# A hybrid decoder trunk on one core: 14 of 16 differential heads' weights transposed by DVE and by way of DRAM

## The chip, the cores and the metric

The kernel runs on one core of a Trainium2 chip. The metric is the device time of one launch in microseconds (us), the median of several runs. Five engines work side by side, each through its own queue in order: PE (TensorE, matmuls; its weight loads are shown as PEld), ACT (ScalarE), DVE (VectorE), POOL (GpSimd) and SP (SyncE). In this kernel SP issues the loads of the weights, and POOL issues most other transfers after the start.

## The reference

The trunk has two layers over 512 tokens of width 2048. In each, one projection of the normed input feeds two groups of eight heads. Group B is a latent attention (MLA). Group A, which the change touches, is a differential attention: each head has two softmax maps over the same values, and their difference weighs the values.

```python
s = jnp.einsum('bqhmd,bkhmd->bmhqk', qb, k).astype(jnp.float32) * scale
...
s = jnp.where((dist >= 0)[None, None, None], s + bias[None, None], NEG_INF)
p = jax.nn.softmax(s, axis=-1)
w = p[:, 0] - lam * p[:, 1]
return jnp.einsum('bhqk,bkhd->bqhd', w.astype(v.dtype), v)
```

The head's output is normed (RMS), scaled, multiplied by a gate, and goes with the other heads' outputs into the output projection. The causal mask means that a block of 128 queries needs only the keys up to its own end.

## The kernel before, in words

**Precision.** Every float32 operand of a matmul is split into a high and a low part of type fp32r: the high one is a cast on ACT, the low one the difference on DVE. A product is three matmuls (`mm3`, L348): high by high, high by low, low by high.

**Weights.** They come in blocks of 128 x 1024 (512 KB) through `WStream` (L62). SP loads `raw` (two buffers), ACT casts `whi` (L104), DVE subtracts to `wlo` (L105), two buffers each. A block is split one block ahead, so the cast waits until PE has left the block before. A block is 24 matmuls of 512 columns.

**Order.** `run_jobs` (L146) walks through a list of jobs, all on PE: projections of 8 steps (`job_proj`, L353), the values' job of 32 steps (`job_v`, L448), parts of the output projection. A step is six matmuls. Attention work is attached to step numbers: `DIFF_AT` (L35) says for a differential head at which steps of its stretch the scores (S), the transposes (T), the products with the values (A) and the norm (F) are issued, for four query blocks (S, T) or key blocks (A). PE, SP and POOL keep this order as written; on ACT and DVE a scheduler may set the order at build time. Each engine then runs its own queue strictly in order, so POOL and SP are not tied to PE's steps: they run ahead until something makes them wait.

**A differential head** h has the jobs z(h) (the gate), q and k of head h+1, and at heads 0 and 4 the values' job for the next four heads, which before the change comes right after z(h). `after` (L57) adds the length of the head's jobs to A and F, so these fall into z(h+1). The steps (L779 to L831):

- `s_step` issues four matmuls into two PSUM banks (tag `s`, two buffers), two softmaxes (`softmax`, L695: DVE L699, ACT L701, DVE L702), scales one map on ACT (L797) and adds the other on DVE (L799). The sum stands in `s1` (tag `sb`, two buffers); `s0` has tag `sa`, two buffers, so the third query block needs the first one's buffers back.
- `t_step` calls `transpose_w` (L705): up to four PE transposes of 128 x 128 into PSUM (L708), ten in a head, then the high part on ACT (L714) and the low part on DVE (L715), into `pth` and `ptl`, one buffer each, which hold the transposed weights of all query blocks.
- `av_step` (L717) issues twelve matmuls in four groups, all of which read `pth` or `ptl`, and at the end prepares the sum of squares (`ones_sum`, tag `kr`, two buffers).
- `fin` is the norm: two matmuls (L342, L343), `rsqrt_of`, two products on DVE (L825, L826), a split.

The last head of each layer has its own steps, `LAST_AT`, since the output projection follows. POOL loads a head's bias at step 0 of the head before it (`load_bias`, L877).

Of the kernel before, what the change touches and what calls it, by code (L numbers as in the profile page):

```python
# [15 lines left out]
P = 128  # L16
T = 512
# [14 lines left out]

MLA_AT = {"S": (2.5, 3.5, 4.5, 7), "T": (5, 7, 9.5, 11), "A": (0.5, 1, 1.5, 5)}
FIRST_AT = {"S": (2.5, 3.5, 8.5, 8), "T": (4.5, 7, 10.5, 11), "A": (0.5, 0.5, 1.5, 5)}
DIFF_AT = {"S": (3, 4, 6, 10), "T": (8.5, 9, 13, 17), "A": (0.5, 1, 2, 2), "F": 5}  # L35
LAST_AT = {"S": (2, 4, 6, 10), "T": (7, 9, 13.5, 17), "A": (18.5, 19, 19.5, 20), "F": 23}


# [124 lines left out]
def trunk(ctx, tc, blocks, xf, gains, diff_lambda, rel_bias_table, onehot, tables, wb, outf):  # L163
# [553 lines left out]
    def av(h, kb):  # L717
# [7 lines left out]
        nc.tensor.matmul(o, vh, h["pl"][:, r], start=False, stop=False)  # L725
        nc.tensor.matmul(o, vl, h["ph"][:, r], start=False, stop=kb == 3)  # L726

    def new_pt(h):
        h["ph"] = t_([P, PTW], F32R, "pth", 1)
        h["pl"] = t_([P, PTW], F32R, "ptl", 1)  # L730
# [46 lines left out]
        return schedule(at, s_step, t_step, av_step)  # L777

    def diff_steps(l, hd, done, at):  # L779
        h = {"e": hd % 4}  # L780

        def s_step(qb):
            def f():
                if qb == 0:
                    h.update(q=st["q"], k=st["k"], b=st["bias"][hd])
                n = (qb + 1) * P
                c = slice(qb * P, (qb + 1) * P)
                p0, p1 = p_("s", 2), p_("s", 2)
                q, (k, kx) = h["q"], h["k"]
                nc.tensor.matmul(p0[:, :n], q[:, 0, c], k[:, 0, :n], start=True, stop=False)  # L790
                nc.tensor.matmul(p1[:, :n], q[:, 1, c], k[:, 1, :n], start=True, stop=False)
                nc.tensor.matmul(p0[:, :n], q[:, 0, c], kx[:, 0, :n], start=False, stop=True)
                nc.tensor.matmul(p1[:, :n], q[:, 1, c], kx[:, 1, :n], start=False, stop=True)
                bias = h["b"][:, 384 - qb * P:]
                s0, m0 = softmax(p0, n, bias, 0.125, "sa")
                s1, m1 = softmax(p1, n, bias, 0.125, "sb")
                nc.scalar.activation(out=s0[:, :n], in_=s0[:, :n], func=AF.Copy, scale=m0[:, 1:2])  # L797
                nc.vector.tensor_tensor(out=m1[:, 1:2], in0=m1[:, 1:2], in1=nlam[:, l:l + 1], op=ALU.mult)
                nc.vector.scalar_tensor_tensor(out=s1[:, :n], in0=s1[:, :n], scalar=m1[:, 1:2], in1=s0[:, :n], op0=ALU.mult, op1=ALU.add)  # L799
                h[qb] = s1  # L800
            return f

        def t_step(qb):
            def f():
                if qb == 0:
                    new_pt(h)
                transpose_w(h, qb, h.pop(qb))
            return f

        def av_step(kb):  # L810
# [17 lines left out]
            split2(m, r)  # L828
            done(m)

        return schedule(at, s_step, t_step, av_step) + [(at["F"], fin)]  # L831


    nlam = sb.tile([P, 120], F32, name="nlam")
# [80 lines left out]
    for l in range(DEPTH):  # L915
# [36 lines left out]
        def v_diff(q, wi=wi):  # L952
            return job_v([b_kouter(wi, C_V + q * T, j) for j in range(8)], lambda kc: (xh[kc], xl[kc]), True)
# [60 lines left out]
        for h in range(NH):  # L1014
            bias = [(0, lambda h=h: [load_bias(i) for i in ((0, 1) if h == 0 else (h + 1,)) if i < NH])]
            jobs = [z_job(C_Z + h * P)]
            if h < NH - 1:
                jobs += ([v_diff(h // 4)] if h % 4 == 0 else []) + d_jobs(h + 1)
                add(jobs, bias, diff_steps(l, h, keep(h), after(DIFF_AT, sum(n for n, _ in jobs))))
            else:  # L1020
                jobs += [job_out_half(l, 0, accs, mslot), job_out_half(l, 1, accs, mslot), job_out_half(l, 2, accs, mslot), job_out_first(l, accs, mslot, last_evac if last else out_evac, spare(0))]
                add(jobs, [(0, load_res(0)), (0, load_res(1)), (22, load_res(2)), (24, load_res(3))] + [(MIX_AT + MIX_ST * i, split_mix(i)) for i in range(8)],
                    diff_steps(l, h, keep(h), LAST_AT))
# [111 lines left out]
```

## Time and profile before

| what | value |
|---|---|
| median of 3 runs | 1797.67 us (1795.96 to 1799.13) |
| the profiled execution's own time | 1796.06 us |
| its span | 1794.3 us |
| PE busy | 1777.7 us, 99% |
| DVE, ACT, POOL busy | 1021.7, 878.4, 41.6 us |
| mean load on the DMA | 101 GB/s |

The profile shows one execution, and its span is 1.76 us shorter than that execution's own time. "Busy" adds up the durations that the profile gives. PE's matmuls are pipelined and overlap: the timeline shows one of 512 columns starting every 0.23 us with a duration of 0.39 us. What an instruction costs PE is therefore read from the starts of its neighbours, not from its duration.

### The profile page before, as it was taken

The page shows a single profiled execution, that of the slowest core. Times are in us where ns is not written, and L with a number is a line of the kernel's source. Part 1 is how long each engine was busy: PE and PEld are TensorE (multiplying, and loading weights), DVE is VectorE, ACT ScalarE, POOL GpSimd, SP SyncE. Part 2 cuts the span into 40 slices and gives each one's busy share as a digit, 9 for nine tenths or more (in the row PEclk, how much of TensorE's full clock was granted, in tenths as well). Part 3 has the DMA queues.
Part 4 walks back from the last instruction along what each step waited for, and adds up shares of the span by engine and source line. Part 5 has one row for each costly group of instructions (what it writes and reads, how often), then busy time and mean ns, then how long its engine had stood idle before and what let it go on. Part 6 is the DMA issues. An engine that isn't in the chain of part 4 may idle for free.

```text
span 1794.3 us, 21822 instructions
## 1 busy us (share of the span) xinstructions
PE 1777.7 (99%) x8341; PEld 1483.6 (83%) x8341; DVE 1021.7 (57%) x1905; ACT 878.4 (49%) x1548; POOL 41.6 (2%) x82
## 2 busy tenths in 40 slices
PE   9999999999999999999999999999999999999997
PEld 7888888888888888888888888888888888888886
DVE  6666646546766477534535655655367745774334
ACT  6455646535555367423434655554256635663331
POOL 0000000000000000001100000000000000000000
PEclk9999999999999999999999999999999999999999
DMA  6342222232322322444432222222332232223343
GB/s 220 99 148 77 65 77 85 85 100 88 91 89 89 103 78 87 129 141 141 141 112 94 82 71 77 79 86 89 99 92 91 77 100 83 90 93 118 118 124 128
DMA packets 55540, 181.13 MB, mean 101 GB/s; under 512 B 6563, under 2 KB 10915, under 8 KB 55436
## 3 DMA queue, kind: packets, MB, share of 16 engines
q1 hardware_dynamic: 48972, 159.10, 28.3%
q0 software_dynamic: 6032, 20.21, 3.8%
q8 instruction: 66, 1.08, 0.3%
q10 hardware_dynamic: 432, 0.43, 0.1%
q14 instruction: 38, 0.31, 0.1%
HBM read 171.30 MB, written 11.03 MB: 102 GB/s over the span
## 4 chain that ended last, share of the span: by engine, by line
PE 97%; DVE 1%; ACT 1%; DMA 0%; issue 0%; SPq 0%; DVEq 0%
PE pacc L349 24%; PE pacc L351 24%; PE pacc L350 24%; PE pacc L464 3%; PE pacc L466 3%; PE pacc L465 3%; PE ptp L708 2%; PE po L725 1%; PE po L726 1%; PE po L724 1%; PE po L464 1%; PE po L466 1%; PE po L465 1%; PE ps L351 1%; PE ps L350 1%; PE ps L349 1%
## 5 line engine op out<-in xcount | busy, mean ns | idle before, releaser
L104 ACT CAST whi<-raw 128x1024 fp32r<-128x1024 f32 (+1 forms) x283 | 292.7, 1035 | 591.5 <-PE pacc L350 412.2
L349 PE MATMUL pacc<-x,whi 128*128 128x512 f32 x1471 | 581.8, 395 | 0.0
L351 PE MATMUL pacc<-x,wlo 128*128 128x512 f32 x1471 | 572.2, 389 | 0.0
L350 PE MATMUL pacc<-x,whi 128*128 128x512 f32 x1471 | 571.8, 389 | 0.0
L105 DVE TENSOR_TENSOR wlo<-raw,whi 128x1024 fp32r<-128x1024 f32 (+1 forms) x283 | 340.9, 1205 | 304.3 <-ACT whi L104 297.2
L351 PEld LDWEIGHTS pacc<-x,wlo 128*128 128x128 f32 x1471 | 276.2, 188 | 59.6
L349 PEld LDWEIGHTS pacc<-x,whi 128*128 128x128 f32 x1471 | 277.0, 188 | 50.1 <-issue 0.2
L350 PEld LDWEIGHTS pacc<-x,whi 128*128 128x128 f32 x1471 | 276.8, 188 | 49.7
L349 PE MATMUL pacc<-mb,whi 128*128 128x512 f32 (+1 forms) x400 | 156.4, 391 | 0.0
L351 PE MATMUL pacc<-mb,wlo 128*128 128x512 f32 (+1 forms) x400 | 154.5, 386 | 0.6 <-DVE wlo L105 0.6
L350 PE MATMUL pacc<-mb,whi 128*128 128x512 f32 (+1 forms) x400 | 154.1, 385 | 0.0
L701 ACT ACTIVATE sa<-sa,m 128x128 f32<-128x128 f32 (+3 forms) x128 | 71.8, 561 | 118.0 <-DVE m L699 117.0
L699 DVE CUSTOM_DVE_ANT_0 sa<-ps,cs 128x128 f32<-128x128 f32 (+3 forms) x128 | 62.3, 486 | 81.1 <-PE ptp L708 30.3
L575 DVE TENSOR_TENSOR tmp<-pacc,rstd 128x512 f32<-128x512 f32 x64 | 44.1, 689 | 94.6 <-PE pacc L351 94.6
L351 PEld LDWEIGHTS pacc<-mb,wlo 128*128 128x128 f32 x400 | 75.2, 188 | 16.7 <-DVE wlo L105 1.5
L350 PEld LDWEIGHTS pacc<-mb,whi 128*128 128x128 f32 x400 | 75.3, 188 | 14.4
L349 PEld LDWEIGHTS pacc<-mb,whi 128*128 128x128 f32 x400 | 75.1, 188 | 14.0
L714 ACT CAST pth<-ptp 128x128 fp32r<-128x128 f32 (+3 forms) x128 | 53.6, 419 | 45.9 <-PE ptp L708 45.6
L464 PE MATMUL pacc<-whi,x 128*128 128x512 f32 x192 | 75.9, 395 | 0.0
L466 PE MATMUL pacc<-whi,x 128*128 128x512 f32 x192 | 74.8, 390 | 0.0
L465 PE MATMUL pacc<-wlo,x 128*128 128x512 f32 x192 | 74.8, 389 | 0.0
L715 DVE TENSOR_TENSOR ptl<-ptp,pth 128x128 fp32r<-128x128 f32 (+3 forms) x128 | 61.6, 484 | 4.4 <-ACT pth L714 2.5
(261 smaller groups left out, 2345.7 us busy)
## 6 DMA issues: line engine op xcount, KB each, us to landing
raw<-in_blocks_dram SPq DMA_DIRECT2D x281, 512.0 KB, 3.5
cs<-brow POOLq DMA_DIRECT2D x16, 256.0 KB, 2.9
cs<-in_x_dram POOLq DMA_DIRECT2D x16, 256.0 KB, 4.3
cs<-xres POOLq DMA_DIRECT2D x16, 256.0 KB, 2.9
out_dram<-x SPq DMA_DIRECT2D x16, 256.0 KB, 2.2
mb<-in_x_dram SPq DMA_DIRECT2D x7, 512.0 KB, 6.8
raw<-in_blocks_dram SPq DMA_DIRECT2D x10, 256.0 KB, 2.6
brow<-brow POOLq DMA_DIRECT2D x8, 320.0 KB, 7.3
```

Of the source, the lines that this page charges most:

```text
L104: nc.scalar.copy(out=a[:, c], in_=r[:, c])
L105: nc.vector.tensor_tensor(out=b[:, c], in0=r[:, c], in1=a[:, c].bitcast(F32), op=ALU.subtract)
L349: nc.tensor.matmul(acc, wh, rh, start=first, stop=False)
L350: nc.tensor.matmul(acc, wh, rl, start=False, stop=False)
L351: nc.tensor.matmul(acc, wl, rh, start=False, stop=last)
L464: nc.tensor.matmul(accs[t], xhi[:, c], hi[:, w], start=kc == 0, stop=False)
L465: nc.tensor.matmul(accs[t], xhi[:, c], lo[:, w], start=False, stop=False)
L466: nc.tensor.matmul(accs[t], xlo[:, c], hi[:, w], start=False, stop=kc == n - 1)
L699: nc.vector.tensor_tensor_reduce(out=s[:, :n], in0=ps[:, :n], in1=bias, scale=-scale, scalar=3.0e38, op0=ALU.add, op1=ALU.min, accum_out=m ...
L701: nc.scalar.activation(out=s[:, :n], in_=s[:, :n], func=AF.Exp, scale=-1.0, bias=m[:, 0:1], accum_out=m[:, 1:2])
L714: nc.scalar.copy(out=view(h["ph"]), in_=pv)
L715: nc.vector.tensor_tensor(out=view(h["pl"]), in0=pv, in1=f32(view(h["ph"])), op=ALU.subtract)
```

## The change

For the heads 0 to 6 of each layer (those with `DIFF_AT`, which now has an entry R), the ten PE transposes of a head are left out. In their place:

- `turn`, in `s_step`: DVE transposes every 32 x 32 block of the weights into `s0`, with the blocks put in another order, and POOL issues four DMAs, one for each 32 partitions, that write them to a DRAM tile `turned` (one for each query block, two sets). Each DMA writes 128 runs of 128, 256, 384 or 512 bytes, by query block.
- `turned_back`, at the steps R: POOL issues one DMA that reads the block back, now transposed, into an SBUF tile with tag `kr` (two buffers). It needs all four writes landed.
- `split_w`, at the steps T: ACT and DVE make the high and low part out of this tile instead of out of PSUM.

T goes from (8.5, 9, 13, 17) to (11.5, 15.5, 18.5, 25.5), A from (0.5, 1, 2, 2) to (3, 3.5, 4, 4) and F from 5 to 6.5 steps behind the head's jobs. The values' job of heads 0 and 4 goes behind the q and k of the next head.

```diff
--- before.py
+++ after.py
@@ -32,7 +32,7 @@
 
 MLA_AT = {"S": (2.5, 3.5, 4.5, 7), "T": (5, 7, 9.5, 11), "A": (0.5, 1, 1.5, 5)}
 FIRST_AT = {"S": (2.5, 3.5, 8.5, 8), "T": (4.5, 7, 10.5, 11), "A": (0.5, 0.5, 1.5, 5)}
-DIFF_AT = {"S": (3, 4, 6, 10), "T": (8.5, 9, 13, 17), "A": (0.5, 1, 2, 2), "F": 5}
+DIFF_AT = {"S": (3, 4, 6, 10), "R": (5, 7, 9, 10.5), "T": (11.5, 15.5, 18.5, 25.5), "A": (3, 3.5, 4, 4), "F": 6.5}
 LAST_AT = {"S": (2, 4, 6, 10), "T": (7, 9, 13.5, 17), "A": (18.5, 19, 19.5, 20), "F": 23}
 
 
@@ -725,6 +725,31 @@
         nc.tensor.matmul(o, vh, h["pl"][:, r], start=False, stop=False)
         nc.tensor.matmul(o, vl, h["ph"][:, r], start=False, stop=kb == 3)
 
+    def turn(h, qb, w, x):
+
+
+        n = (qb + 1) * P
+        nc.vector.transpose(out=x[:, :n].rearrange("p (b k j) -> p b k j", b=4, j=32), in_=w[:, :n].rearrange("p (k b j) -> p b k j", b=4, j=32))
+        d = turned[h["hd"] % 2][qb]
+        for a in range(4):
+            nc.gpsimd.dma_start(out=d[:, :, a, :].rearrange("b i r -> i b r"), in_=x[a * 32:(a + 1) * 32, :n].rearrange("i (b r) -> i b r", b=4))
+
+    def turned_back(h, qb):
+        t = t_([P, T], F32, "kr", 2)
+        nc.gpsimd.dma_start(out=t[:, :(qb + 1) * P], in_=turned[h["hd"] % 2][qb].rearrange("b i a r -> (b i) (a r)"))
+        return t
+
+    def split_w(h, qb, t):
+        n = (qb + 1) * P
+
+        def view(x):
+            return x.rearrange("p (b a c) -> p b a c", a=4, c=32)[:, qb:4 * qb + 1:3, :, :]
+        pv = t[:, :n].rearrange("p (a k c) -> p k a c", a=4, c=32)
+        nc.scalar.copy(out=view(h["ph"]), in_=pv)
+        nc.vector.tensor_tensor(out=view(h["pl"]), in0=pv, in1=f32(view(h["ph"])), op=ALU.subtract)
+
+    turned = [[dram.tile([4, 32, 4, 32 * (qb + 1)], F32, name=f"turned{i}_{qb}") for qb in range(4)] for i in range(2)]
+
     def new_pt(h):
         h["ph"] = t_([P, PTW], F32R, "pth", 1)
         h["pl"] = t_([P, PTW], F32R, "ptl", 1)
@@ -777,7 +802,7 @@
         return schedule(at, s_step, t_step, av_step)
 
     def diff_steps(l, hd, done, at):
-        h = {"e": hd % 4}
+        h = {"e": hd % 4, "hd": hd}
 
         def s_step(qb):
             def f():
@@ -797,14 +822,20 @@
                 nc.scalar.activation(out=s0[:, :n], in_=s0[:, :n], func=AF.Copy, scale=m0[:, 1:2])
                 nc.vector.tensor_tensor(out=m1[:, 1:2], in0=m1[:, 1:2], in1=nlam[:, l:l + 1], op=ALU.mult)
                 nc.vector.scalar_tensor_tensor(out=s1[:, :n], in0=s1[:, :n], scalar=m1[:, 1:2], in1=s0[:, :n], op0=ALU.mult, op1=ALU.add)
-                h[qb] = s1
+                if "R" in at:
+                    turn(h, qb, s1, s0)
+                else:
+                    h[qb] = s1
             return f
 
         def t_step(qb):
             def f():
                 if qb == 0:
                     new_pt(h)
-                transpose_w(h, qb, h.pop(qb))
+                if "R" in at:
+                    split_w(h, qb, h.pop(qb))
+                else:
+                    transpose_w(h, qb, h.pop(qb))
             return f
 
         def av_step(kb):
@@ -828,7 +859,13 @@
             split2(m, r)
             done(m)
 
-        return schedule(at, s_step, t_step, av_step) + [(at["F"], fin)]
+        def r_step(qb):
+            def f():
+                h[qb] = turned_back(h, qb)
+            return f
+
+        back = [(at["R"][qb], r_step(qb)) for qb in range(4)] if "R" in at else []
+        return schedule(at, s_step, t_step, av_step) + back + [(at["F"], fin)]
 
 
     nlam = sb.tile([P, 120], F32, name="nlam")
@@ -1015,7 +1052,7 @@
             bias = [(0, lambda h=h: [load_bias(i) for i in ((0, 1) if h == 0 else (h + 1,)) if i < NH])]
             jobs = [z_job(C_Z + h * P)]
             if h < NH - 1:
-                jobs += ([v_diff(h // 4)] if h % 4 == 0 else []) + d_jobs(h + 1)
+                jobs += d_jobs(h + 1) + ([v_diff(h // 4)] if h % 4 == 0 else [])
                 add(jobs, bias, diff_steps(l, h, keep(h), after(DIFF_AT, sum(n for n, _ in jobs))))
             else:
                 jobs += [job_out_half(l, 0, accs, mslot), job_out_half(l, 1, accs, mslot), job_out_half(l, 2, accs, mslot), job_out_first(l, accs, mslot, last_evac if last else out_evac, spare(0))]
```

## Rows read from the trace of the kernel before

**Rows 1.** The page: busy us of each engine, share of the span, instructions.

```profile
PE 1777.7 (99%) x8341; PEld 1483.6 (83%) x8341; DVE 1021.7 (57%) x1905; ACT 878.4 (49%) x1548; POOL 41.6 (2%) x82
```

**Rows 2.** The page: the chain that ended last, by engine.

```profile
PE 97%; DVE 1%; ACT 1%; DMA 0%; issue 0%; SPq 0%; DVEq 0%
```

**Rows 3.** The waits of PE: total us, times, longest us.

```profile
PE ps L391 <- DVE x L294: 2.2, 1, 2.2
...
PE pacc L351 <- DVE wlo L105: 0.6, 2, 0.3
```

**Rows 4.** Groups by form, PE: us in all, mean ns | idle before.

```profile
L708 PE MATMUL ptp<-ident,sa 128*128 128x128 f32 x160 | 28.0, 275 | 0.0
L708 PE MATMUL ptp<-ident,sb 128*128 128x128 f32 x160 | 25.6, 272 | 0.0
```

**Rows 5.** Timeline of PE, head 2: start us, duration us, line.

```profile
481.11 0.39 PE L350 MATMUL pacc<-x,whi 128*128 128x512 f32 x1
...
484.74 0.39 PE L351 MATMUL pacc<-x,wlo 128*128 128x512 f32 x1
484.97 0.49 PE L708 MATMUL ptp<-ident,sb 128*128 128x128 f32 x3
...
488.05 0.39 PE L349 MATMUL pacc<-x,whi 128*128 128x512 f32 x1
...
490.54 0.39 PE L351 MATMUL pacc<-x,wlo 128*128 128x512 f32 x1
490.77 0.60 PE L708 MATMUL ptp<-ident,sb 128*128 128x128 f32 x4
...
494.44 0.39 PE L351 MATMUL pacc<-x,wlo 128*128 128x512 f32 x1
```

**Rows 6.** Heads 3, 4: us, busy PE, PEld, DVE, ACT, POOL; clock, DMA share, GB/s.

```profile
506.80:545.70 38.90, 38.90 (x186) 32.55 (x185) 27.76 (x61) 23.63 (x47) 0.54 (x1) 1.00 0.29 89
545.70:628.20 82.50, 82.50 (x378) 68.49 (x377) 40.47 (x73) 34.66 (x58) 0.54 (x1) 1.00 0.30 93
```

**Rows 7.** Groups by form, DVE: the sum of both maps, widest and narrowest.

```profile
L799 DVE SCALAR_TENSOR_TENSOR sb<-sb,m,sa 128x512 f32<-128x512 f32 x16 | 11.9, 747 | 0.5
...
L799 DVE SCALAR_TENSOR_TENSOR sb<-sb,m,sa 128x128 f32<-128x128 f32 x16 | 5.6, 351 | 1.6
```

**Rows 8.** The line L880 on POOL: duration ns, min/median/max.

```profile
L880 POOL DMA_DIRECT2D cs<-brow x16: 536/538/570, 280.2 to 1447.2; - x16
```

**Rows 9.** DMA issues: count, KB each, median us from issue to landing.

```profile
raw<-in_blocks_dram SPq DMA_DIRECT2D x281, 512.0 KB, 3.5
cs<-brow POOLq DMA_DIRECT2D x16, 256.0 KB, 2.9
...
brow<-brow POOLq DMA_DIRECT2D x8, 320.0 KB, 7.3
...
xres<-tmp POOLq DMA_DIRECT2D x8, 256.0 KB, 2.3
...
tab<-in_rel_bias_table_dram SPq DMA_DIRECT2D x1, 1.0 KB, 3.8
```

**Rows 10.** Timeline of all engines, head 3.

```profile
506.81 0.22 PE L790 MATMUL ps<-ka,qa 128*128 128x128 f32 x1
...
509.18 0.35 DVE L799 SCALAR_TENSOR_TENSOR sb<-sb,m,sa 128x128 f32<-128x128 f32 x1
...
518.84 0.39 PE L790 MATMUL ps<-ka,qa 128*128 128x512 f32 x1
...
518.86 1.22 DVE L105 TENSOR_TENSOR wlo<-raw,whi 128x1024 fp32r<-128x1024 f32 x1
...
522.44 1.06 ACT L104 CAST whi<-raw 128x1024 fp32r<-128x1024 f32 x1 [1.69 <-PE pacc L350]
...
526.40 0.74 DVE L799 SCALAR_TENSOR_TENSOR sb<-sb,m,sa 128x512 f32<-128x512 f32 x1
```

**Rows 11.** The waits of DVE: total us, times, longest us.

```profile
DVE sa L699 <- PE ptp L708: 30.3, 14, 2.2
```

## The prediction, made before the changed kernel was run

> **What bounds the kernel now.** I read the busy shares first. PE is busy for 99% of the span; DVE has 43% of it free, ACT half, and POOL does almost nothing [rows 1]. The chain that ended last runs through PE for 97% [rows 2]. The waits of PE then tell whether it is fed late anywhere: the longest entry is 2.2 us at the start, and all its waits for weight parts come to 0.6 us [rows 3]. So TensorE is full from end to end, and the time changes by what is taken from it or by what makes it wait. By stretch, head 3 lasts 38.9 us and head 4, with the values' job, 82.5 us, PE busy throughout at the full granted clock, the level of 2.4 GHz [rows 6].
>
> **What the removed transposes cost PE.** Their 272 ns [rows 4] overlap their neighbours, so I go by starts. Sixteen matmuls of 512 columns from 481.11 to 484.74 take 3.63 us, 0.227 us each. From 484.74 to 488.05 thirteen such matmuls and three transposes start: 3.31 - 13 x 0.227 = 0.36 us for the three. From 490.54 to 494.44, fifteen and four transposes: 3.90 - 15 x 0.227 = 0.50 us [rows 5]. That includes the few matmuls behind each group that come slightly slower. A head has ten: query blocks 0 and 1 go together as three, block 2 has three, block 3 four. So 2 x 0.36 + 0.50 = 1.22 us a head, and 14 x 1.22 = 17.1 us. Lower bound: by 0.11 us for one transpose and none for its followers, 140 x 0.11 = 15.4 us. The upper bound by busy time, 140 x 0.272 = 38 us, is excluded by the starts; I keep 20 us, for followers that I didn't count.
>
> **What DVE and ACT get.** The trace has no DVE transpose. The nearest rows are other DVE instructions of the same widths, such as the sum of the maps: 747 ns at 512 columns, 351 at 128 [rows 7], some 2.2 us for the four widths of a head. Bounds: nothing, if it were to displace an idle moment, and twice that. I take 2.2 us. The split keeps its two instructions and its size and only changes its source. In the short head DVE goes from 27.8 to 30 us of some 37.7, ACT stays at 23.6 [rows 6]: busy, not full. Before, DVE also sat waiting for PE's transposes to give back an `sb` buffer, 14 times, up to 2.2 us [rows 11]. That wait goes, since DVE itself frees the buffer now. What is late next is the other buffer, `sa`: it is free when its four writes have landed. PE lost nothing to the old wait.
>
> **What POOL and the DMA engines get.** A head issues 16 writes and 4 reads. POOL needs 0.54 us to issue one [rows 8], so 11 us in a head of 38 us; the transfers that stand on that queue before (a bias in each head) are needed a head later, or are not due for many steps, and lose nothing. A round trip is four issues (2.2 us), a landing, one issue and a landing. The landing of a short-run write is not in the trace. Nearest: 2.3 us (`xres` to DRAM) and 2.9 us (bias from DRAM, also with POOL); far ends: 3.8 us for the table with runs of 32 bytes, and 7.3 us for the copy from DRAM to DRAM [rows 9]. I take 2.9 us for each, the slower of the two that share queue and direction, and keep 2.3 and 7.3. The new bytes, 2 x 0.66 MB a head, add some 34 GB/s to 89, or about 0.11 to a DMA share of 0.29 [rows 6]; if the short runs cost three times as much, the share is still near 0.6. Weights land in 3.5 us [rows 9] and are loaded about two blocks (11 us) ahead, so that covers it.
>
> The Trainium skill ("DMA: Bandwidth & Descriptors", Specifications) puts line rate at transfers of 512 B or more; below that, it says, the engine reads, modifies and writes. Three of the four query blocks write shorter runs, so by it their writes land later than the 2.9 us that I take, while the fourth block's don't. No run here shows such a write. It speaks for the second rival below.
>
> **Does the transposed block come in time?** I count from PE's start of a head's first scores. By the trace the sum of the first block starts 2.4 us later (506.81 to 509.18) and takes 0.35 us, and the sum of the last block is ready 8.3 us behind its scores (518.84 to 526.40, plus 0.74) [rows 10]. After the change, the last block's scores come at 12.7 us: seven steps of 1.36 us, and 3.1 us of scores, products and norm in between. Its sum is ready at 21.0, turned by DVE at 21.8, written at 24.0 + 2.9 = 26.9, read back at 27.4 + 2.9 = 30.3, split at 31.6. The products begin a head later, just before the next head's scores: 38.9 - 1.2 - 0.7 = 37.0 us. That leaves 5.4 us. Earlier blocks have more, and POOL's order holds no circle: the third read waits for a `kr` buffer that the first block's split gives back, and for its own writes, both before the last block is turned.
>
> **The new waits on DVE and ACT.** The first block's writes land at 2.8 + 0.35 + 2.2 + 2.9 = 8.2 us, the third block's softmax wants that `sa` from 6.8 us on: DVE may wait 1.4 us, less than the 2.2 us that it waited before at no cost. Behind it in DVE's queue are the weights' low parts. One ends at 520.08, and PE takes up that block when the cast after it is let go, at 522.44 [rows 10]: about 2.3 us of cover there. The four splits of a head wait in the same way for their read, with the same cover. If the cover is gone, PE waits by the excess.
>
> **The v job, A and F.** They are the same matmuls in another order. The values' job now starts behind the k projection and takes that one's PSUM bank as its last, 2 us after its end; before, it did the same behind the gate. I cost it at nothing, between -1 and +2 us for the four of them, since the evacuation that covers it takes one DVE instruction.
>
> **Sum.** 1796.06 - 17.1 = 1779.0 us for the profiled execution's own time. The median is 1.6 us above that execution, so I predict 1780.6 us, with a range of its own from 1776 (gain 20, nothing lost) to 1786 (five us of small waits).
>
> **Rivals.**
>
> *Partly eaten.* Most splits come in time, but some heads lose a few tenths of a us to one or two blocks whose weight parts come late. For it: in the first 20 us of a head DVE is close to full, and the change puts 2.2 us more there and moves the norm 1.5 steps nearer to the gate's work. Against: 2.2 us of waiting cost nothing before [rows 11, 3]. At 0.3 to 0.6 us a head, 4 to 8 us are lost: 1785 to 1789 us.
>
> *Slower: the weight parts queue behind a wait for DRAM.* The split of a turned block stands in ACT's and DVE's queues ahead of a weight block's cast or subtraction. If write and read land 1.5 us later each than the queue's order allows for, the two add up to 3 us against a cover of 2.3; 0.7 us for each of four blocks and 14 heads is 39 us: 1820 us. It decides the sign where PE loses 1.22 us a head, that is where a round trip is 2.6 us late. For it: 3.8 us in [rows 9] is 1.5 above 2.3. Against: the queues' order can be set for the later landing, and a wait further up in the queue uses up lateness for all behind it.
>
> *No change.* The lost waits come to 1.0 to 1.5 us a head by chance, or PE's gaps are filled again because DVE sets the pace of the first half: about 1797 us.
>
> **How the numbers follow.** Chances: forecast 0.60, partly eaten 0.20, no change 0.07, slower 0.13. What a measurement of this kernel can tell from no change is about 0.2%, 3.6 us: faster means under 1794.1. Faster is the first two cases, 0.80; the same 0.07; slower 0.13. The range takes in the first two cases, with 5 us above the second for a price of a wait that I have no row for: 1776 to 1794 us.
>
> **What would show it.** Right: no L708 row with `sb` but for the two last heads (20 instead of 160); PE's waits still of a few us; heads of about 37.7 us between first scores; DVE transposes near 0.2 to 0.75 us; reads landing under 4 us; the waits of ACT for the turned tile short. Wrong, partly eaten or slower: PE waits for `wlo` or `whi` of L104 and L105, or for `pth` and `ptl` at L724 and L725, in the differential heads, with ACT or DVE waiting for a DMA before it. Wrong in the size: heads that are shorter by other than 1.2 us with no waits at all.

## The result, and the profile after

The changed kernel takes 1819.83 us (median, 1817.65 to 1821.60) beside 1796.82 us for the kernel before on the same chip: a ratio of 1.0128, 95% interval 1.0116 to 1.0140. The forecast was 1780.6 us, faster; the kernel became 23 us slower. The profiled span grew from 1794.3 to 1817.8 us. Lines behind L724 have moved: L815 to L818 (the scores) were L790 to L793, and L824 (the sum of the maps) was L799. The runs e1, e5 and e9 have the numbers of the kernel before.

The page after: busy times as in [rows 1], the chain that ended last as in [rows 2], and the DMA queue that POOL issues to (packets, MB, share).

```profile
PE 1777.9 (98%) x8201; PEld 1476.7 (81%) x8201; DVE 1051.3 (58%) x1961; ACT 881.6 (48%) x1548; POOL 194.8 (11%) x362
...
q0 software_dynamic: 16336, 38.58, 7.1%
...
PE 72%; DVE 10%; DMA 7%; ACT 6%; issue 3%; POOL 2%; DVEq 0%; POOLq 0%; SPq 0%; ACTq 0%
```

PE has 140 instructions less, as it should, and the same busy time. Busy time doesn't show what was won: some matmuls ran at the lower clock and lasted longer, and at each stall the end of a matmul, which otherwise overlaps the next (0.39 us against a start every 0.23), counts in full. The chain is the clearer sign: it ran through PE for 97%, now for 72%, and the other 28% goes through DVE, DMA, ACT, issue and POOL. The groups of instructions that the change made (us in all, mean ns | idle before, releaser), with the answer to [rows 4]:

```profile
L735 POOL DMA_DIRECT2D turned<-sa x224 | 122.3, 553 | 591.9 <-ACT whi L104 388.9
...
L732 DVE STREAM_TRANSPOSE sa<-sb 128x128 f32<-128x128 f32 (+3 forms) x56 | 28.5, 509 | 1.4
...
L749 DVE TENSOR_TENSOR ptl<-kr,pth 128x128 fp32r<-128x128 f32 (+3 forms) x56 | 26.9, 480 | 56.5 <-ACT pth L748 56.5
L748 ACT CAST pth<-kr 128x128 fp32r<-128x128 f32 (+3 forms) x56 | 25.4, 454 | 70.3 <-DMA kr<-turned 70.1
...
L708 PE MATMUL ptp<-ident,sb 128*128 128x128 f32 x20 | 3.5, 272 | 0.0
```

DVE's transposes take 28.5 us over 14 heads, 2.0 us a head against the 2.2 assumed. The 56 splits are cheap (25.4 us on ACT), but ACT stands idle 70.3 us before them, waiting for the read. The DMA issues (KB each, median us from issue to landing), which answer to [rows 9]:

```profile
raw<-in_blocks_dram SPq DMA_DIRECT2D x281, 512.0 KB, 3.5
cs<-brow POOLq DMA_DIRECT2D x16, 256.0 KB, 3.9
...
turned<-sa POOLq DMA_DIRECT2D x56, 64.0 KB, 2.0
kr<-turned POOLq DMA_DIRECT2D x14, 256.0 KB, 3.6
```

In the median the round trip costs about what was assumed: 2.0 us for the largest write and 3.6 for the largest read, where 2.9 stood for each, and the weights still land in 3.5 us. The smaller writes landed in 1.9 us (48 KB), 1.8 (32 KB) and 3.1 (16 KB). The waits of PE after (total us, times, longest), beside [rows 3]:

```profile
PE pacc L351 <- DVE wlo L105: 11.2, 16, 1.0
PE pacc L464 <- DVE tmp L575: 3.1, 1, 3.1
PE ps L816 <- ACT x L287: 2.3, 2, 1.1
...
PE ps L816 <- DVE ka L687: 1.8, 3, 0.8
```

And three waits of ACT and DVE, the last of them the entry of [rows 11], unchanged:

```profile
ACT pth L748 <- DMA kr<-turned: 70.1, 27, 7.7
```

```profile
DVE sa L699 <- DMA turned<-sa: 19.4, 13, 3.0
...
DVE sa L699 <- PE ptp L708: 30.3, 14, 2.2
```

PE waits for weight parts, once for the evacuation of a projection (L575), and for the parts of k at a head's first scores; before, the wait for weight parts came to 0.6 us in all, and the other two were not among its five longest entries. Heads 3 and 4 in windows, first scores to first scores, as [rows 6]; the third line is the stretch behind the 3.1 us wait:

```profile
507.30:546.30 39.00, 38.13 (x175) 31.57 (x174) 29.60 (x66) 23.88 (x46) 11.49 (x21) 1.00 0.41 120
546.30:635.30 89.00, 84.81 (x367) 69.60 (x366) 43.02 (x78) 34.88 (x58) 11.50 (x21) 0.96 0.32 100
...
586.20:590.00 3.80, 3.80 (x9) 3.03 (x10) 3.64 (x5) 2.35 (x4) 0.00 (x0) 0.50 0.42 125
```

The short head lasts 39.0 us where 37.7 was expected; head 4 lasts 89.0 us instead of 82.5 before. In head 4 of the first layer the timeline shows the whole mechanism (start, duration, releaser of the wait before it):

```profile
572.66 2.20 POOL L735 DMA_DIRECT2D turned<-sa  x4 [5.65 <-DVE ptl L749]
579.97 0.57 POOL L739 DMA_DIRECT2D kr<-turned  x1 [5.12 <-issue]
...
584.11 0.62 ACT L748 CAST pth<-kr 128x512 fp32r<-128x512 f32 x1 [7.69 <-DMA kr<-turned]
584.63 1.04 ACT L104 CAST whi<-raw 128x1024 fp32r<-128x1024 f32 x1
584.75 0.69 DVE L749 TENSOR_TENSOR ptl<-kr,pth 128x512 fp32r<-128x512 f32 x1 [7.08 <-ACT pth L748]
585.36 0.69 DVE L575 TENSOR_TENSOR tmp<-pacc,rstd 128x512 f32<-128x512 f32 x1
586.10 0.80 PE L464 MATMUL pacc<-whi,x 128*128 128x512 f32 x1 [3.12 <-DVE tmp L575]
586.70 0.63 PE L465 MATMUL pacc<-wlo,x 128*128 128x512 f32 x1
587.12 0.63 PE L466 MATMUL pacc<-whi,x 128*128 128x512 f32 x1
```

The last split of head 4 stands on ACT and DVE **ahead** of the evacuation of k (L575). ACT waits 7.7 us for the read, DVE 7.1 us for ACT, k's PSUM bank stays taken, and the values' job wants it as its last bank. PE stands still for 3.1 us, and then its matmuls start every 0.43 us instead of 0.23: the granted clock is 0.50, the lower level of 1.2 GHz, until 592.2.

Part of ACT's wait is peculiar to this head. Its four writes landed 2.0 to 2.8 us after their issue, the last at 576.7, but POOL issued the read only at 579.97, 3.2 us later; in the other heads it is mostly 0.6 us. The profile names no releaser ("issue"). The same gap stands in this head in e7, e12 and e15, and not in head 4 of the second layer, which lasts 86.9 us, without that stall; its cause stays open.

In the short head 3 the split's wait does little:

```profile
528.18 1.04 ACT L104 CAST whi<-raw 128x1024 fp32r<-128x1024 f32 x1
...
530.83 0.74 DVE L824 SCALAR_TENSOR_TENSOR sb<-sb,m,sa 128x512 f32<-128x512 f32 x1
...
530.97 0.51 PE L351 MATMUL pacc<-x,wlo 128*128 128x512 f32 x1 [0.84 <-DVE wlo L105]
...
532.09 0.70 DVE L732 STREAM_TRANSPOSE sa<-sb 128x512 f32<-128x512 f32 x1
...
537.61 0.56 POOL L739 DMA_DIRECT2D kr<-turned  x1 [2.03 <-DMA turned<-sa]
...
541.07 0.62 ACT L748 CAST pth<-kr 128x512 fp32r<-128x512 f32 x1 [3.88 <-DMA kr<-turned]
...
546.95 0.33 PE L818 MATMUL ps<-mb,qa 128*128 128x128 f32 x1 [0.18 <-DVE mb L689]
```

A weight cast stands behind the last softmax (528.18), its low part comes late and PE waits 0.84 us. That is ten us before the last split, and e10 and e11 show that it doesn't come from a read. Behind the split stand the parts of k, for which the first scores wait 0.18 us here (up to 1.2 elsewhere).

### The profile page after: what moved, and what is told of

It reads as the page before. It is cut to its first block, busy times and chain, and to the rows that moved or that the text cites. A ratio compares the mean times of both kernels' runs of the same rounds, so it can differ in the third digit from the quotient of the medians.

```text
span 1817.8 us, 22291 instructions
## 1 busy us (share of the span) xinstructions
PE 1777.9 (98%) x8201; PEld 1476.7 (81%) x8201; DVE 1051.3 (58%) x1961; ACT 881.6 (48%) x1548; POOL 194.8 (11%) x362
## 4 chain that ended last, share of the span: by engine, by line
PE 72%; DVE 10%; DMA 7%; ACT 6%; issue 3%; POOL 2%; DVEq 0%; POOLq 0%; SPq 0%; ACTq 0%
PE pacc L349 17%; PE pacc L351 17%; PE pacc L350 16%; DMA turned<-sa 4%; PE pacc L465 3%; PE pacc L464 3%; PE pacc L466 3%; DMA kr<-turned 3%; DVE wlo L105 2%; POOL turned L735 2%; ACT whi L104 1%; PE ptp L708 1%; PE po L465 1%; PE po L464 1%; PE po L466 1%
## 5 line engine op out<-in xcount | busy, mean ns | idle before, releaser
L735 POOL DMA_DIRECT2D turned<-sa x224 | 122.3, 553 | 591.9 <-ACT whi L104 388.9
L699 DVE CUSTOM_DVE_ANT_0 sa<-ps,cs 128x128 f32<-128x128 f32 (+3 forms) x128 | 62.4, 488 | 107.7 <-PE ptp L708 30.3
L749 DVE TENSOR_TENSOR ptl<-kr,pth 128x128 fp32r<-128x128 f32 (+3 forms) x56 | 26.9, 480 | 56.5 <-ACT pth L748 56.5
L748 ACT CAST pth<-kr 128x128 fp32r<-128x128 f32 (+3 forms) x56 | 25.4, 454 | 70.3 <-DMA kr<-turned 70.1
```

The costliest lines, as they stand in the source:

```text
L699: nc.vector.tensor_tensor_reduce(out=s[:, :n], in0=ps[:, :n], in1=bias, scale=-scale, scalar=3.0e38, op0=ALU.add, op1=ALU.min, accum_out=m ...
L735: nc.gpsimd.dma_start(out=d[:, :, a, :].rearrange("b i r -> i b r"), in_=x[a * 32:(a + 1) * 32, :n].rearrange("i (b r) -> i b r", b=4))
L749: nc.vector.tensor_tensor(out=view(h["pl"]), in0=pv, in1=f32(view(h["ph"])), op=ALU.subtract)
```

## The experiments

Each run was timed beside the kernel before on the same chip (medians 1796.1 to 1797.3 us); ratios carry 95% intervals. They came in four groups. The diffs show the lines that make the difference; what a run shares with an earlier one is named in its text, and lines that only hand on a name are left out. In e2, e6, e10, e11, e13 and e14 some or all splits read a resident tile instead of the turned weights, so their products are made from other numbers; the sizes are the same.

### First group: moves, waits, blocks or weights?

**e1_moves**, the kernel before with the three moves alone:

```diff
-DIFF_AT = {"S": (3, 4, 6, 10), "T": (8.5, 9, 13, 17), "A": (0.5, 1, 2, 2), "F": 5}
+DIFF_AT = {"S": (3, 4, 6, 10), "T": (8.5, 9, 13, 17), "A": (3, 3.5, 4, 4), "F": 6.5}
-jobs += ([v_diff(h // 4)] if h % 4 == 0 else []) + d_jobs(h + 1)
+jobs += d_jobs(h + 1) + ([v_diff(h // 4)] if h % 4 == 0 else [])
```

> The kernel before with the moves alone: products at 3, 3.5, 4, 4 and norm at 6.5 steps, values' job behind the next head's q and k; the ten PE transposes stay at their steps, no DRAM. Theory 'wait' (splits of a turned block hold ACT's and DVE's queues until the read has landed, and weight parts and evacuations behind them come late): no DRAM, no loss, 1797 us, within 4. Rival 'crowd' (the norm now falls into the last block's softmax and the gate's work, so DVE and ACT are late with no DRAM at all): 1810 to 1837 us, the upper end if it makes up all of the 40 us that the changed kernel lost.

Measured: 1822.81 us, 1.0153 [1.0136, 1.0169]. It looks as if the moves explained all, but the waits of PE say otherwise:

```profile
PE ptp L708 <- DVE sb L799: 19.3, 12, 1.6
PE ps L791 <- DVE ka L687: 2.3, 2, 1.1
```

The first line is a wait that the changed kernel cannot have: PE's own transposes, at their old steps, come before a sum that the moved norm has delayed. Nearly equal times with different waits; e5 takes this one out.

**e2_no_read_wait**, the kernel after with all splits reading a resident tile; writes and reads are still issued:

```diff
-        pv = t[:, :n].rearrange("p (a k c) -> p k a c", a=4, c=32)
+        pv = rstd[0][:, :n].rearrange("p (a k c) -> p k a c", a=4, c=32)
```

> The changed kernel, but the splits take a resident tile in place of the block that was read back (so the products with the values work on other numbers); DVE transposes, writes and reads are all still issued. Theory 'wait': the queues no longer hold, 1779 to 1786 us. Rival 'crowd': the same instructions at the same places on DVE and ACT, 1805 us or more. A third outcome, near 1820, would say that the transfers themselves disturb the weights' loads.

Measured: 1794.95 us, 0.9992 [0.9983, 1.0002]. Some 24 us go with the read. But the removed dependency also let the build-time order put all splits far ahead, right behind the head's first softmaxes, so this run took away a wait *and* moved an instruction. e10 and e11 separate the two.

**e3_three_blocks**, the last and widest query block stays with PE; products, norm and values' job at the old places, the first three splits at 11.5, 13 and 15 steps:

```diff
-                if "R" in at:
+                if "R" in at and qb < 3:
```

> Only query blocks 0 to 2 go by way of DRAM, block 3 is transposed by PE; products, norm and values' job at their places of before. Six of ten transposes leave PE: 14 x 0.72 = 10 us at most. Both theories: the products are needed 10 us and more after the third block's read, and nothing is moved, so 1787 to 1792 us. If 'wait' holds for the earlier blocks too, each of which the splits may wait for: 1797 or more.

Measured: 1808.54 us, 1.0067 [1.0052, 1.0082]. Waits of 6.8 us for `wlo`, 5.7 and 2.9 at the start of the values' job: three blocks by way of DRAM still lose more than they win. How much of that is their splits' wait this run doesn't tell; e10 and e11 do, for the places of the kernel after.

**e4_weights_first**, the kernel after with the weights' cast and subtraction ahead in ACT's and DVE's order:

```diff
-            self._split(self.ns)
+            with self.tc.high_priority(): self._split(self.ns)
```

> The changed kernel, with the weights' casts and subtractions given priority when the order of ACT and DVE is made; nothing else. 'Wait': an in-order queue that stands before a read still holds what is behind it, and the evacuations are not helped; 1810 to 1822 us. 'Crowd': the weight parts no longer stand behind the softmax, 1785 to 1800 us.

Measured: 1829.17 us, 1.0181 [1.0166, 1.0196]. The waits for `wlo` nearly vanish and others take their place, the products' first of all:

```profile
PE po L725 <- DVE ptl L749: 19.2, 8, 3.1
PE pacc L464 <- DVE tmp L575: 2.6, 2, 1.8
PE ps L815 <- DVE ka L687: 2.5, 2, 1.3
```

The order of ACT and DVE alone moves the time by 10 us, in the wrong direction here.

### Second group: the moves and the bank

**e5_moves_late_t**, e1 with the transposes late enough for the sum:

```diff
-DIFF_AT = {"S": (3, 4, 6, 10), "T": (8.5, 9, 13, 17), "A": (3, 3.5, 4, 4), "F": 6.5}
+DIFF_AT = {"S": (3, 4, 6, 10), "T": (8.5, 9, 16, 21), "A": (3, 3.5, 4, 4), "F": 6.5}
```

> The run with the moves alone lost time because PE reached the transposes of the third block before the sum of its maps was ready. Here the same moves, with the transposes of the blocks 2 and 3 at 16 and 21 steps in place of 13 and 17, so PE need not wait for a sum. If the later norm costs only by that wait: 1797 to 1802 us. If crowding of DVE and ACT delays the weight parts by itself, as theory 'crowd' says: 1805 to 1815 us.

Measured: 1801.96 us, 1.0033 [1.0020, 1.0046]. The moves cost 6 us. The main new wait is `ps L791 <- DVE ka L687`, 1.1 us at the first scores of the last head of each layer, with slower matmuls behind it.

**e6_old_places**, e2 with A, F and the values' job at their old places:

```diff
-DIFF_AT = {"S": (3, 4, 6, 10), "R": (5, 7, 9, 10.5), "T": (11.5, 15.5, 18.5, 25.5), "A": (3, 3.5, 4, 4), "F": 6.5}
+DIFF_AT = {"S": (3, 4, 6, 10), "R": (5, 7, 9, 10.5), "T": (11.5, 13, 15, 17), "A": (0.5, 1, 2, 2), "F": 5}
-jobs += d_jobs(h + 1) + ([v_diff(h // 4)] if h % 4 == 0 else [])
+jobs += ([v_diff(h // 4)] if h % 4 == 0 else []) + d_jobs(h + 1)
```

> The run whose splits take a resident tile, with products, norm and values' job put back to their places of before (splits at 11.5, 13, 15, 17 steps). It tells what the moves cost when nothing waits for a read. 'Crowd' by the moves: back to 1779 to 1784 us, all of the 17 us of the transposes. If the DVE transposes and the writes crowd DVE instead: it stays near 1795 us.

Measured: 1790.26 us, 0.9971 [0.9959, 0.9983]; 3.8 us less than e2 by the ratios, so the moves cost about as much here as in e5.

**e7_bank**, the kernel after, where the values' job takes its last PSUM bank from another tag and the last head's first scores come a step later:

```diff
-LAST_AT = {"S": (2, 4, 6, 10), "T": (7, 9, 13.5, 17), "A": (18.5, 19, 19.5, 20), "F": 23}
+LAST_AT = {"S": (3, 4, 6, 10), "T": (7, 9, 13.5, 17), "A": (18.5, 19, 19.5, 20), "F": 23}
-accs = [p_("acc", 3), p_("o", 1), p_("acc", 3), p_("acc", 3)]
+accs = [p_("acc", 3), p_("o", 1), p_("acc", 3), p_("acc", 3) if scaled_by is None else p_("tp", 2)]
```

> The changed kernel; the values' job takes its last PSUM bank from the tag of the transposes, which the differential heads hardly use now, in place of the bank of the k projection before it; and the last head's first scores come at step 3 in place of 2, behind the first product. Theory 'wait', by the heads' lengths: the heads 4 lose 6.5 and 4.5 us more than without the read's wait, the heads 0 some 1.5 each and the last heads some 2 each, since the last split holds the evacuation of k. If the bank is the place: 1803 to 1810 us. If not, 1817 us or more.

Measured: 1810.15 us, 1.0072 [1.0055, 1.0089]. The 3.1 us stall and its slow stretch are gone: 10 us of 23 came from two due times. The one in head 4 the split had pushed past; the one of the last heads' first scores the moves alone make late, as e5 shows without any read.

**e8_later**, e4 and e7 together, with products and norm later:

```diff
-DIFF_AT = {"S": (3, 4, 6, 10), "R": (5, 7, 9, 10.5), "T": (11.5, 15.5, 18.5, 25.5), "A": (3, 3.5, 4, 4), "F": 6.5}
+DIFF_AT = {"S": (3, 4, 6, 10), "R": (5, 7, 9, 10.5), "T": (11.5, 15.5, 18.5, 25.5), "A": (4.5, 5, 5, 5), "F": 7}
```

> The run with the weights first, with that bank and that step, and products at 4.5 and 5 and the norm at 7 steps. With the weights first, PE waited for the last split (19 us) and no longer for weight parts; 1.5 to 2 steps more cover 2 to 2.7 us of up to 3.1 each. If that is all: 1785 to 1800 us, under the kernel before or equal to it. If the later norm only crowds more: 1810 us or more.

Measured: 1808.79 us, 1.0063 [1.0039, 1.0086]. Now 12.6 us of waits stand at the first scores, for the parts of k (`ps L816 <- DVE ka L687` 10.3 us in 10 waits): on ACT the last split's cast is still ahead of the casts of k's parts.

### Third group: which split, and its place

**e9_last_step**, e5 with the last heads' first scores a step later:

```diff
-LAST_AT = {"S": (2, 4, 6, 10), "T": (7, 9, 13.5, 17), "A": (18.5, 19, 19.5, 20), "F": 23}
+LAST_AT = {"S": (3, 4, 6, 10), "T": (7, 9, 13.5, 17), "A": (18.5, 19, 19.5, 20), "F": 23}
```

> e5 (the moves alone, with PE's transposes set late enough) lost 5.9 us against the kernel before, and its trace shows waits only at the first scores of the last head of each layer, 1.1 us each with about 3.6 us of slower matmuls behind them. This run starts those scores one step later. Theory that the moves cost nothing else: ratio 0.999 to 1.000, 1795 to 1797 us. Rival, that the moves cost by crowding DVE in every head: 1800 us or more, the ratio stays above 1.002.

Measured: 1797.79 us, 1.0010 [1.0001, 1.0019]. All but 1.8 us of what the moves cost by themselves lay in the last heads' first scores; what is left is 0.1%, hardly clear of noise.

**e10_last_no_wait**, the kernel after where only the last split reads the resident tile, held behind q's evacuation:

```diff
-split_w(h, qb, h.pop(qb))
+with (tc.issue_after(st["aq"].ins) if qb == 3 else ExitStack()), (tc.issue_after(st["eq"].ins) if qb == 3 else ExitStack()): split_w(h, qb, h.pop(qb))
-pv = t[:, :n].rearrange("p (a k c) -> p k a c", a=4, c=32)
+pv = (rstd[0] if qb == 3 else t)[:, :n].rearrange("p (a k c) -> p k a c", a=4, c=32)
```

(`aq` and `eq` are the last ACT and DVE instructions of q's evacuation; `issue_after` sets the order in the queue alone, and adds no wait for a result.)

> The kernel after; only the last split of each head (the four-block one) reads a resident tile, so it never waits for a read from DRAM, and it is held at its old place in ACT's and DVE's order, behind q's evacuation and ahead of k's. The output is made from other weights. Theory that the wait of this one split holds up k's evacuation and the weight parts: 1793 to 1800 us. Rival, all four splits' waits share the loss: 1806 to 1814 us. Second rival, that e2 gained because its splits, free of a wait, were put much earlier in the order: 1814 us or more here.

Measured: 1805.17 us, 1.0045 [1.0030, 1.0059]: the kernel after takes 0.0083 or 15 us more, and 14 of its 56 splits make the difference. Only in the heads 0 is the split's place the same as in the kernel after; in the other twelve it stands one weight block earlier, so the wait and the place went together there. Nothing else in ACT's and DVE's order differs. Between first scores the profiled executions show where the time went: the heads 0 are 1.0 and 1.2 us shorter, the heads 4 6.6 and 2.9 us (82.4 us instead of 89.0 in the first layer), the stretches of the last two heads of each layer 1.3 to 1.6 us each, and the short heads 1, 2, 3 and 5 no shorter on the whole (head 3: 38.90 us instead of 39.05). The time lies between the two theories' ranges: the wait is the largest term, but not all. PE still waits for weight parts as before:

```profile
PE pacc L351 <- DVE wlo L105: 11.4, 15, 1.0
```

**e11_all_no_wait**, the same for all four splits, the first three held behind the weight block that is split last before them:

```diff
+with tc.issue_after((st["aq"] if qb == 3 else ws.last[0]).ins), tc.issue_after((st["eq"] if qb == 3 else ws.last[1]).ins): split_w(h, qb, h.pop(qb))
+pv = rstd[0][:, :n].rearrange("p (a k c) -> p k a c", a=4, c=32)
```

> As e10, but all four splits of a head read the resident tile, each held near its place of the kernel after. Theory of the last split: within 3 us of e10. Rival, all four waits: 1793 to 1798 us, at least 8 us below e10. Second rival, the place in the order and the added instructions on ACT and DVE: within 3 us of e10, and both at 1812 us or more.

Measured: 1803.34 us, 1.0039 [1.0025, 1.0054], within 2 us of e10, and 11.0 us of waits for `wlo` with no split waiting for a read. The three earlier splits' waits cost nothing that stands clear of noise, and the late weight parts don't come from the reads. The distance from e11 to e2, 8.4 us, is the order alone: in e2 the same splits stand earlier, out of the crowded part, and some instructions around them moved too.

**e12_behind_k**, e7 with the last split, which reads the turned weights again, held behind k's evacuation, and A and F as in e8:

```diff
+with (tc.issue_after(st["ak"].ins) if qb == 3 else ExitStack()), (tc.issue_after(st["ek"].ins) if qb == 3 else ExitStack()): split_w(h, qb, h.pop(qb))
```

> A true version: e7 (the values' job takes another PSUM bank, the last head's scores one step later) with the last split held behind k's evacuation on ACT and DVE, and the next head's products 1 to 1.5 steps later, the norm at 7. Theory that what the wait holds up is what counts: k's evacuation is free of it, so the first scores and the values' job come in time, 1794 to 1802 us. Rival, the wait only moves on to the weight parts behind the split in the next head, or the products come too late: 1808 us or more, as e7.

Measured: 1802.46 us, 1.0037 [1.0024, 1.0050], half a us above what the theory gave. ACT's wait for the read falls from 70.1 to 6.0 us; what stays is mainly 10.4 us for `wlo`, once a head.

### Fourth group: the removed work by itself, and a version that wins

**e13_pe_only**, the kernel before without the 140 transposes; the splits read a resident tile, written at e6's steps, and nothing goes to DRAM. As an edit of e6:

```diff
-        nc.vector.transpose(out=x[:, :n].rearrange("p (b k j) -> p b k j", b=4, j=32), in_=w[:, :n].rearrange("p (k b j) -> p b k j", b=4, j=32))
...
-            nc.gpsimd.dma_start(out=d[:, :, a, :].rearrange("b i r -> i b r"), in_=x[a * 32:(a + 1) * 32, :n].rearrange("i (b r) -> i b r", b=4))
...
-        nc.gpsimd.dma_start(out=t[:, :(qb + 1) * P], in_=turned[h["hd"] % 2][qb].rearrange("b i a r -> (b i) (a r)"))
```

> The kernel before with one thing changed: the 140 PE transposes of the 14 heads are left out, and the splits read a resident tile from SBUF; no DVE transpose, no write, no read, all places as before. The output is made from other weights. Prediction's term: 17.1 us less, 1779 to 1781 us, ratio 0.9905. Rival, the transposes cost PE only their 0.11 us: 15.4 us less, 1781 us. Second rival, PE's gain is taken back by other waits even so: 1785 us or more.

Measured: 1779.98 us, 0.9902 [0.9885, 0.9918]. That is 17.6 us, where the prediction had 17.1.

**e14_no_dma**, e13 with DVE's 56 transposes back, the first line of that diff, and still no DMA.

> As e13 with the 56 DVE transposes put back (some 2.0 us of DVE per head), no writes and no reads. e6, which has the DMAs too, took 1790.3 us. Theory that the rest of e6's loss is DVE being crowded where the values' job and the weight parts need it: 1787 to 1791 us. Rival, that it is the DMAs (the sums' buffers held until the writes land, memory traffic): within 2 us of e13.

Measured: 1779.52 us, 0.9903 [0.9888, 0.9918]. DVE's transposes cost nothing that these runs can see; my theory that they crowd DVE falls. e6 differs from this run by its DMAs, and by the order that a scheduler makes of them, and is 12 us slower by the ratios, 8 us in the profiled executions, half of that in the heads 0. The timelines of head 0 show where. e14, the third block's softmax, then the gate's evacuation:

```profile
355.24 0.52 DVE L699 CUSTOM_DVE_ANT_0 sa<-ps,cs 128x384 f32<-128x384 f32 x1
...
358.29 0.68 DVE L575 TENSOR_TENSOR tmp<-pacc,rstd 128x512 f32<-128x512 f32 x1
```

e6, the same two, the four writes of the first block, and the values' job:

```profile
351.65 2.21 POOL L735 DMA_DIRECT2D turned<-sa  x4 [68.91 <-ACT whi L104]
...
357.25 0.56 DVE L699 CUSTOM_DVE_ANT_0 sa<-ps,cs 128x384 f32<-128x384 f32 x1 [2.31 <-PE pacc L351]
...
360.33 0.68 DVE L575 TENSOR_TENSOR tmp<-pacc,rstd 128x512 f32<-128x512 f32 x1
...
361.07 0.50 PE L464 MATMUL pacc<-whi,x 128*128 128x512 f32 x1 [1.86 <-DVE tmp L575]
```

Four issues of 0.55 us, then a landing (2.8 us in the median for the 16 KB writes in this window), and only then is the first block's `sa` free. The third softmax wants it 2.3 us earlier. The profile puts that wait down to PE, but the block's last scores had started at 354.07; without the writes (e14) the wait isn't there. The gate's evacuation behind it is 2.0 us late, and so is the values' job.

**e15_both**, e12 with the weights' cast and subtraction given priority within the heads 0 to 5 of each layer (as built, `diff` is set for these):

```diff
-            self._split(self.ns)
+            with (self.tc.high_priority() if self.diff else ExitStack()): self._split(self.ns)
```

> e12 with the weights' cast and subtraction given priority in ACT's and DVE's order within the differential heads 0 to 6. e12's trace still has 10.4 us of PE waiting for the weights' low parts, once a head, and 0.8 us a head at the first scores. Theory that the order alone makes these: the 10.4 us go, 1789 to 1794 us, under the kernel before. Rival, what is put behind them (splits, scores' softmax) becomes the next wait, as in e4: 1802 us or more.

Measured: 1788.62 us, 0.9951 [0.9936, 0.9966]. With the last split out of the way, nearly the same edit that lost 10 us in e4 wins 15 by the ratios.

**e16_step**, e15 with the first two scores a step later:

```diff
-DIFF_AT = {"S": (3, 4, 6, 10), "R": (5, 7, 9, 10.5), "T": (11.5, 15.5, 18.5, 25.5), "A": (4.5, 5, 5, 5), "F": 7}
+DIFF_AT = {"S": (4, 5, 6, 10), "R": (6, 7, 9, 10.5), "T": (11.5, 15.5, 18.5, 25.5), "A": (4.5, 5, 5, 5), "F": 7}
```

> e15 with the first two scores of a head one step later (4 and 5), so that k's evacuation has 1.4 us more. Theory that 0.8 us a head are lost there: 8 to 10 us less than e15. Rival, that the last block's sum or the softmax buffers then come later and the loss only moves: no better than e15.

Measured: 1784.91 us, 0.9930 [0.9915, 0.9945]: 12.4 us under the kernel before, with the 140 transposes gone from PE and all 280 DMAs of the change issued. The gain over e15 is 3.7 us, not the 8 to 10 expected. Heads 3 and 4 of it, and what PE still waits for weight parts:

```profile
505.00:542.61 37.61, 37.61 (x175) 31.60 (x174) 29.74 (x66) 23.67 (x46) 11.46 (x21) 1.00 0.41 124
542.61:623.75 81.14, 81.14 (x368) 67.67 (x367) 42.61 (x78) 34.85 (x59) 11.46 (x21) 1.00 0.36 112
```

```profile
PE pacc L351 <- DVE wlo L105: 1.8, 3, 1.1
```

The short head lasts 37.61 us, the 37.7 that the prediction had for the change itself, with DVE as busy as in the kernel after (29.7 and 29.6 us).

### The terms put together

By the ratios, against 1797 us; each difference is uncertain by 3 to 4 us (95%), so the terms of 0.2 and 1.1 us can't be told from nothing.

| step | from, to | us |
|---|---|---|
| PE's transposes gone | before, e13 | -17.6 |
| DVE's transposes | e13, e14 | +0.2 |
| writes and reads issued, buffers held until they land, ACT's and DVE's order with them | e14, e6 | +12.2 |
| products, norm and values' job later | e6, e2 | +3.8 |
| splits at their late place on ACT and DVE | e2, e11 | +8.4 |
| the first three splits wait for their reads | e11, e10 | +1.1 |
| the last split waits for its read (in 12 heads one weight block later, too) | e10, after | +14.9 |
| all | before, after | +23.0 |

The terms are not independent. With another order on ACT and DVE, another PSUM bank for the values' job and two steps, e16 pays all but some 5 us of them off (0.9930 beside 0.9902 of e13).

## Why the prediction was wrong

**The step that failed** is in "The new waits on DVE and ACT" and "Does the transposed block come in time?": the four splits "wait in the same way for their read, with the same cover", and the last block is judged by one due time only, that of its products. So these waits entered the sum with nothing. The runs show in its place that the last split's wait is paid by what stands *behind* it on two engines that run strictly in order. That was k's evacuation, with two due times of its own: the next head's first scores and, in heads 0 and 4, the values' job. Neither was followed up. The products themselves were in time: in head 3 the split was done 35.1 us after the first scores (541.73 + 0.69 - 507.27) and the products came at 38.4; the 5.4 us to spare had shrunk to about 3. With its place one block later, that wait costs 14.9 us (e10 to the kernel after), most of it in the heads 4 and nothing that shows in the short heads. Putting k ahead of it, with products and norm later, gains 6 us (e7 to e12), and the weights first on top of that 15 more (e15).

**The last block's sum** was taken as ready 8.3 us after its scores, from the kernel before [rows 10]. After, it is 11.1 us: scores at 520.44, sum at 530.83 + 0.74. The moved norm and the splits now stand in that stretch. A duration read from a chain on a shared engine doesn't outlive a change that puts work on it.

**The wait for `sa`** was sized well: 1.4 us foreseen, 1.5 on average and up to 3.0 measured (19.4 us in 13 waits). It was costed at nothing by a misreading of [rows 11]. Those 14 waits are not of the differential heads: in the kernel before they stand between 162 and 318 us and between 1046 and 1202 us, in the latent heads (group B), ahead of each layer's first differential scores (at 346.8 us in the first layer). The change doesn't touch them, and the kernel after has the same 30.3 us in 14 waits. So the row says nothing of what a wait costs in a differential head. There, as e6 shows in head 0, the gate's evacuation stands behind it and the values' job behind that. With the other effects of the DMAs this is the 12.2 us of the third term.

**The values' job, A and F** were costed at -1 to +2 us; 3.8 (e6 to e2) and 6 us (e5) were measured, nearly all of the latter in the first scores of the last heads (e9), a place that the prediction didn't look at; `LAST_AT` wasn't edited. The shared bank was named there, as covered by "one DVE instruction"; it was, until that instruction stood behind a wait for DRAM.

**The clock** was not a term at all. Behind the longer stalls of PE the granted clock fell to one half: in head 4 fourteen matmuls started every 0.43 us instead of 0.23, 2.9 us lost on top of the 3.1. Three more stretches of some 3.4 us, at the last head of each layer and in head 4 of the second, had the same clock of 0.50.

**Right:** the 17.1 us (17.6 in e13), which rested on starts and not on busy time; DVE's transposes, 2.0 us a head and free (e14); POOL's 0.55 us an issue; the landings in the median; the undisturbed weights; a head of 37.7 us once nothing waits (37.61 in e16).

**The rivals.** "Slower", priced at 1820 us, has the right time and a mechanism that is right only in kind. It asked for round trips 3 us later than assumed, with weight parts behind them, and spread 0.7 us over each of four splits and 14 heads. Landings were late by that much only in head 4 of the first layer, where POOL issued the read late; the weight parts stayed late by 11 us with no read to wait for (e10, e11); and three of the four splits cost about 1 us together. The time that agrees is in part luck. "Partly eaten" named weight parts that come late in a crowded start of the head. They do, for 11.2 us in 16 waits, more than its 4 to 8; but e15 shows that the order made them late, not a full DVE: with the same DVE work they are nearly gone.

**Short writes.** The Trainium skill ("DMA: Bandwidth & Descriptors", Specifications) puts line rate at transfers of 512 B or more. No row before the change could tell what that does here. Now rows do: in the median, writes in runs of 256 and 384 bytes landed in 1.8 and 1.9 us, no later than those of 512 bytes (2.0). Those of 128 bytes took 3.1 us, but two of the four of a block often landed in 1.7 (head 3: 1.7 to 3.7), so whether the run length or another transfer makes that isn't shown.

## What to carry to other kernels

When a wait for a transfer is put into an engine that runs in order, list everything behind it on that engine, and the due time of each, before asking whether the waited-for result itself is in time. Where a build-time scheduler sets that order, the step number at which an instruction is written says little, and pinning one instruction behind the urgent one can be worth more than a faster transfer. A run that removes a dependency also frees the scheduler to move the instruction: compare the orders first, and hold the place when the question is the wait.

## What was not expected of the hardware

A short stall of PE costs more than itself, but not always. After 3.1 us in head 4, and after three waits of 0.49, 1.14 and 0.22 us within 3 us at the last head of the first layer, the granted clock was 0.50 for 6 and some 3.5 us. After single waits of 0.8 to 1.0 us for `wlo`, as in head 3, it stayed at full speed. In e10's profiled execution two waits of 1.24 and 0.96 us within 2 us, and one of 1.14 with 0.22 behind it, left it at full speed too. That execution is the fastest of e10's five (1800.5 to 1808.4 us), and the others ran at a lower mean clock (0.994 to 0.996 against 0.997). Which stalls bring it about, these runs don't settle.
